# Column sums of the first norm on TensorE, and the low-rank projections moved ahead of and among the first rotations

## Chip, cores and metric

The kernel runs on one core of one Trainium2 chip. The metric is the device time of one execution in microseconds (us). The kernel before takes 2462.11 us, the median of three runs (2460.17 to 2463.86). Engines go by their short names: PE is TensorE (PEld its weight loads), DVE VectorE, ACT ScalarE, POOL GpSimd, SP the engine that issues most loads.

## The reference, cut to what matters

The model has several layers on a sequence of 512 with 1024 features: a layer of latent attention and retention, one of gated linear attention, then two more with mixtures of experts. The change lies in the first layer alone:

```python
h = _rmsnorm(x, mix_norm_even[i])
cq, ckv, k_rope, rq, rk, rv, rg = _split(h @ w_in_even[i], EVEN_SPLIT)
a = _mla(cq, ckv, k_rope, positions, ...)
r = _retention(rq, rk, rv, rg, positions, ...)
x = x + jnp.concatenate([a, r], axis=-1) @ w_out_even[i]
```

`cq` (384 features) and `ckv` (256) are the low-rank inputs of the latent attention, `k_rope` 32 more features. `rq` and `rk` are rotated by position, `rv` are the retention's values, `rg` its gates. The retention has eight heads of 64 features; its result is normed by head and multiplied by `silu(rg)`.

## The kernel before

Everything is kept as transposed tiles of 128 features by 512 positions, eight for `x`. A product of two float32 operands is made of three products of operands split in a high and a low part (`mm3`, lines 152 to 156): high by high, high by low, low by high. A weight tile of up to 128x2048 is loaded by SP into one of two `wraw` buffers, ScalarE writes its high part (`whi`, line 147, in three pieces), and VectorE or GpSimd the low part (`wlo`, line 149), in turn by the count of weights (`weight`, line 134).

A tile scheduler sets each engine's order from the order of the code, its own time line and a few hints; buffers are given out by pools. `K.u` gives one of 42 tiles of a ring, `K.h` one of four longer-lived tiles. The PSUM banks are `mm`, `tr`, `sm` and `sc`, two buffers each.

The first layer goes as follows (`layer0`, from line 458). `split_g` scales the eight tiles of `x` by the norm's gains and splits them (`xh`, `xl`). `norm_cols` (line 294) squares the tiles on ScalarE, adds the squares up on VectorE in `acc` (line 220), and `colsum` (line 222) sums `acc` over its partitions with four matmuls against a column of ones, one for each block of 128 positions. `rms_cols` makes the inverse root of it, `rc`, one number for each position. It is not applied to `x`: it goes into the rotation's table `rtab` (line 551), into the copy of the values (`ret_values`, line 531) and into a row `rb` for the gates.

`low_rank` (line 485) is a generator: five projections of 128 features (weights `w_c`), each 24 matmuls of 128x512, with a split of the result (`ch`, `cl`) and its square added to `accq` or `acck`, then `krT` of 32 features. Two of its projections are made ahead of the rotations. `ret_rows` (line 505) makes `rq`, then `rk`, in 16 blocks of 24 matmuls of 128x256: VectorE multiplies a block by cosines and sines (`xc`, `xs`, line 513), GpSimd adds them, PE transposes the result. `ret_values` has eight more blocks. `retention` (line 590) takes the heads in four pairs. For each pair it makes a decay matrix `D` for each head (GpSimd, VectorE, then an Exp on ScalarE, line 599), and in four steps the scores (`sc`, line 606), the scores by decay (`At`, line 608, VectorE) and their product with the values (`sm`, line 613). The norm of the pair follows: squares `s2` on ScalarE, a product with ones by blocks (line 618), `rsqrt_wide` (lines 194 to 204: a logarithm and an Exp on ScalarE, `rwv`, `rwt`, `rwr` on VectorE), the gated result `ro` (lines 621 and 622) and its split `ah`, `al` (lines 258 and 259).

`weave` sets generators beside each other by weights. The retention (20) is woven with the gates and what is left of `low_rank` (8), so those projections fill PE while the other engines work on a pair's norm:

```python
for _ in chain(ret_rows(0, rqT), ret_rows(1, rkT), ret_values()):
    pass
...
weave((retention(), 20), (chain(ret_gates(), low), 8))
```

Of the kernel before, what the change touches and what calls it, by code (L numbers as in the profile page):

```python
# [10 lines left out]
ACT = mybir.ActivationFunctionType  # L11
# [3 lines left out]
P = 128  # L15
# [11 lines left out]
class Ctx:  # L27
# [194 lines left out]
    def colsum(self, acc):  # L222

        ps = self.sm()
        for t in range(4):
            self.summed = self.nc.tensor.matmul(ps[:, t:t + 1], acc[:, t * P:(t + 1) * P], self.ones[:, 0:1], start=True, stop=True).ins
        return ps[:, 0:4]

    def rms_cols(self, acc, n, eps):
# [36 lines left out]
def weave(*parts):  # L266

    live = [[g, n, 0] for g, n in parts]
    while live:
        p = min(live, key=lambda p: p[2] / p[1])  # L270
        p[2] += 1
        try:
            next(p[0])
        except StopIteration:
            live.remove(p)


def chain(*gens):
    for g in gens:
        yield from g  # L280
# [12 lines left out]

def norm_cols(K, xT):

    acc = K.u("acc")
    for k in range(8):
        K.sumsq_add(acc, xT[k], k == 0)
    return K.rms_cols(acc, 1024, 1e-6)


def norm_split(K, xT, g):
# [115 lines left out]
def proj_T(K, src, n, nk, xh, xl):  # L418

    wh, wl = src if isinstance(src, tuple) else K.weight(src, nk * n * P)  # L420
    wh = wh[:, :nk * n * P].rearrange("p (k n) -> p k n", k=nk)
    wl = wl[:, :nk * n * P].rearrange("p (k n) -> p k n", k=nk)
    for j in range(n):
        ps = K.mm()
        for k in range(nk):
            K.mm3(ps, wh[:, k, j * P:(j + 1) * P], wl[:, k, j * P:(j + 1) * P], xh[k], xl[k], k == 0, k == nk - 1)
        yield ps


def proj_N(K, src, n, xh, xl):  # L430

    nk = len(xh)
    wh, wl = K.weight(src, nk * n)
    wh = wh[:, :nk * n].rearrange("p (k n) -> p k n", k=nk)
    wl = wl[:, :nk * n].rearrange("p (k n) -> p k n", k=nk)
    for t in range(4):
        s = slice(t * P, (t + 1) * P)
        ps = K.mm()[:, :n]
        for k in range(nk):
            K.mm3(ps, xh[k][:, s], xl[k][:, s], wh[:, k, :], wl[:, k, :], k == 0, k == nk - 1)  # L440
        yield t, ps


def proj_few(K, src, n, xh, xl):

    wh, wl = (w[:, :8 * n].rearrange("p (k n) -> p k n", k=8) for w in K.weight(src, 8 * n))
    ps = K.mm()[:n]
    for k in range(8):
        K.mm3(ps, wh[:, k, :], wl[:, k, :], xh[k], xl[k], k == 0, k == 7)
    return ps  # L450
# [7 lines left out]
def layer0(K, xT, A, late):  # L458
# [16 lines left out]
    late()  # L475
    xh, xl = split_g(K, xT, g)
    rc0 = norm_cols(K, xT)
    rc = c.tile([P, 4], F32, name="rc")
    V.tensor_copy(out=rc, in_=rc0)
# [5 lines left out]
    def low_rank():  # L485

        for j in range(5):
            ps, = proj_T(K, A["w_c"][j] if j else w_c0, 1, 8, xh, xl)
            h, l = K.ur("ch"), K.ur("cl")
            gg = gq[:, j:j + 1] if j < 3 else gkv[:, j - 3:j - 2]  # L490
            K.split_into(h, l, ps, gg)
            K.sumsq_add(accq if j < 3 else acck, ps, j in (0, 3))
            (cqh if j < 3 else ckh).append(h)
            (cql if j < 3 else ckl).append(l)
            yield
        V.tensor_copy(out=krT, in_=proj_few(K, A["w_kr"], 32, xh, xl))

    low = low_rank()
    for _ in range(2):
        next(low)  # L500


# [2 lines left out]
    def ret_rows(which, dst):  # L505

        for b in range(2):
            for t, ps in proj_N(K, A[("w_rq", "w_rk")[which]][b], 256, xh, xl):
                tabs = rtab[which][:, t]
                p4 = ps.rearrange("p (h b) -> p h b", b=32)  # L510
                xc, xs, xr = (K.u(n)[:, :256] for n in ("xc", "xs", "xr"))
                for o, tab in ((xc, tabs[:, 0]), (xs, tabs[:, 1])):
                    V.tensor_tensor(out=o.rearrange("p (h b) -> p h b", b=32), in0=p4, in1=tab.unsqueeze(1).to_broadcast([P, 8, 32]), op=MU)  # L513
                c4, s4, r4 = (o.rearrange("p (h a b) -> p h a b", a=2, b=32) for o in (xc, xs, xr))
                G.tensor_tensor(out=r4[:, :, 0], in0=c4[:, :, 0], in1=s4[:, :, 1], op=SU)
                x = G.tensor_tensor(out=r4[:, :, 1], in0=c4[:, :, 1], in1=s4[:, :, 0], op=AD)
                if t == 1:
                    first.setdefault("rotation", x.ins)
                pt = K.tr()
                for j in range(2):  # L520
                    nc.tensor.transpose(pt[:, j * P:(j + 1) * P], xr[:, j * P:(j + 1) * P], K.ident)
                for j in range(2):
                    d = dst[2 * b + j]
                    if which:
                        for i, r in enumerate((slice(0, 64), slice(64, P))):
                            K.copy(d[i][r, t * P:(t + 1) * P], pt[r, j * P:(j + 1) * P])
                    else:
                        K.copy(d[:, t * P:(t + 1) * P], pt[:, j * P:(j + 1) * P])
                yield

    def ret_values():
        for b in range(2):
            for t, ps in proj_N(K, A["w_rv"][b], 256, xh, xl):
                x = nc.scalar.activation(out=rv[t][:, b * 256:(b + 1) * 256], in_=ps, func=ACT.Copy, scale=rc[:, t:t + 1])
                first.setdefault("value", x.ins)
                yield

    def ret_gates():
        for b in range(2):
            for ps in proj_T(K, A["w_rg"][b], 2, 8, xh, xl):  # L540
                o = K.u("sg")
                V.tensor_tensor(out=o, in0=ps, in1=rb, op=MU)
                K.silu2(o)
                sg.append(o)
                yield
# [4 lines left out]
        for i, tab in enumerate((cos, sin)):  # L550
            V.tensor_scalar(out=rtab[0][:, t, i], in0=tab[:, t, 16:48], scalar1=rc[:, t:t + 1], scalar2=None, op0=MU)
    V.tensor_scalar(out=rtab[1], in0=rtab[0], scalar1=0.125, scalar2=None, op0=MU)
    rqT, rv = ([K.u("rT") for _ in range(4)] for _ in range(2))
    rkT = [[K.u("rk") for _ in range(2)] for _ in range(4)]
    for x, y in rkT:
        G.memset(x[64:P], 0.0)
        G.memset(y[0:64], 0.0)
    for _ in chain(ret_rows(0, rqT), ret_rows(1, rkT), ret_values()):
        pass


    th = K.load(A["theta"])
# [27 lines left out]
    def retention():  # L590
        for pair in range(4):
            Ds = []
            for h in (2 * pair, 2 * pair + 1):
                D = small.tile([P, 896], F32, tag="D", name="D")
                with K.tc.issue_after(first["rotation"]):
                    G.tensor_scalar(out=D, in0=dp, scalar1=lg[:, h:h + 1], scalar2=None, op0=MU)
                V.scalar_tensor_tensor(out=D, in0=dm, scalar=lg[:, 8 + h:9 + h], in1=D, op0=MU, op1=AD)
                with K.tc.issue_after(first["value"]):
                    nc.scalar.activation(out=D, in_=D, func=ACT.Exp)
                Ds.append(D)  # L600
            po = K.sm()
            for k in range(4):
                At = []
                for i in range(2):
                    ps = K.sc()
                    nc.tensor.matmul(ps, rkT[pair][i][:, k * P:(k + 1) * P], rqT[pair], start=True, stop=True)
                    a = K.u("At")
                    V.tensor_tensor(out=a, in0=ps, in1=Ds[i][:, 384 - 128 * k:896 - 128 * k], op=MU)
                    At.append(a)
                yield  # L610
                for i in range(2):
                    h = 2 * pair + i
                    nc.tensor.matmul(po[i * 64:(i + 1) * 64, :], rv[k][:, h * 64:(h + 1) * 64], At[i], start=k == 0, stop=k == 3)
            s2 = K.u("s2")
            nc.scalar.activation(out=s2, in_=po, func=ACT.Square)
            yield
            pn = K.mm()
            nc.tensor.matmul(pn, bo, s2, start=True, stop=True)
            r = K.rsqrt_wide(pn, 1.0 / 64, 1e-6)
            o = K.u("ro")  # L620
            V.scalar_tensor_tensor(out=o, in0=po, scalar=go[:, pair:pair + 1], in1=sg[pair], op0=MU, op1=MU)
            V.tensor_tensor(out=o, in0=o, in1=r, op=MU)
            ah[4 + pair], al[4 + pair] = K.ur("ah"), K.ur("al")
            K.split_into(ah[4 + pair], al[4 + pair], o)

    rb = K.row_bcast(rc, "rb0")
    weave((retention(), 20), (chain(ret_gates(), low), 8))


    def second(acc, n, nm):  # L630
# [10 lines left out]
    sq = second(accq, 384, "q")  # L641
# [108 lines left out]
    out = lambda half: resid_T(K, xT, A["w_out"][half], ah[half * 4:], al[half * 4:])  # L750
# [1569 lines left out]
```

## Time and profile before

| | |
|---|---|
| median of three runs | 2462.11 us (2460.17 to 2463.86) |
| profiled execution | 2463.21 us, span 2461.1 us |
| mean granted TensorE clock | 0.954 of full speed |
| busy in the span | PE 2241.3 us, DVE 1493.9, ACT 1063.8, POOL 623.0 |

The span runs from the first to the last instruction of the profiled execution; its own time has 2.1 us around that. In the timelines a row is a start, a duration and an instruction, output first; a bracket tells how long its engine was idle before it and what ended that. Rows with a count stand for several alike. Matmuls are pipelined, so durations of neighbours overlap, and the pace is the difference of starts.

### The profile page before, as it was taken

What the parts mean: (1) busy time and instruction counts of PE and PEld (TensorE: products, weight loads), DVE (VectorE), ACT (ScalarE), POOL (GpSimd) and SP (SyncE); (2) the same over time, 40 slices, a digit from 0 to 9 for tenths busy, and PEclk for the clock granted to TensorE, in tenths of its full rate; (3) what the DMA queues carried; (4) which work ended last, traced back from release to release, by engine and by line L of the source; (5) the groups of instructions that cost most, each with busy time, mean ns of one, the idle gap of its engine ahead of it and who ended that gap; (6) DMA issues with size and microseconds to landing.
All of it is one profiled execution on the core that took longest, in us unless ns stands there. A gap on an engine that the chain in (4) does not pass through costs nothing. (4 is left out here: it accounts for less than half of the span.)

```text
span 2461.1 us, 31765 instructions
## 1 busy us (share of the span) xinstructions
PE 2241.3 (91%) x12180; PEld 1820.3 (74%) x12180; DVE 1493.9 (61%) x2866; ACT 1063.8 (43%) x1796; POOL 623.0 (25%) x491
## 2 busy tenths in 40 slices
PE   7999899999999999999999999997883999997892
PEld 6944657888886888788888887576773877786782
DVE  6356865534534656896576354776766445676766
ACT  4333465323325333443243234645664444445563
POOL 6322302222222332000000021124543121124443
PEclk9999999999999999999999999997997999988996
DMA  4100201223222121332333442046884221155884
GB/s 147 70 26 32 93 1 69 98 83 114 87 83 89 69 78 52 103 112 97 135 112 103 153 145 92 35 171 212 329 314 166 95 103 69 69 197 206 305 312 162
DMA packets 71817, 306.67 MB, mean 125 GB/s; under 512 B 18048, under 2 KB 19072, under 8 KB 46048
## 3 DMA queue, kind: packets, MB, share of 16 engines
q1 hardware_dynamic: 61328, 282.29, 32.2%
q0 software_dynamic: 6912, 16.79, 2.0%
q10 hardware_dynamic: 3408, 5.39, 0.7%
q8 instruction: 100, 1.64, 0.3%
q14 instruction: 69, 0.57, 0.1%
HBM read 280.18 MB, written 32.64 MB: 127 GB/s over the span
## 5 line engine op out<-in xcount | busy, mean ns | idle before, releaser
L149 POOL TENSOR_TENSOR wlo<-wraw,whi 128x683 fp32r<-128x683 f32 (+9 forms) x233 | 427.5, 1860 | 973.2 <-ACT whi L147 922.8
L147 ACT ACTIVATE whi<-wraw 128x683 fp32r<-128x683 f32 (+9 forms) x627 | 474.7, 818 | 408.7 <-issue 135.5
L149 DVE TENSOR_TENSOR wlo<-wraw,whi 128x683 fp32r<-128x683 f32 (+9 forms) x394 | 403.4, 1059 | 110.2 <-ACT whi L147 109.7
L154 PE MATMUL mm<-xh,whi 128*128 128x512 f32 (+2 forms) x608 | 242.5, 399 | 10.0 <-ACT xh L261 8.4
L155 PE MATMUL mm<-xl,whi 128*128 128x512 f32 (+2 forms) x608 | 239.8, 394 | 0.2 <-DVE xl L262 0.2
L156 PE MATMUL mm<-xh,wlo 128*128 128x512 f32 (+2 forms) x608 | 239.2, 393 | 0.4 <-POOL wlo L149 0.3
L154 PE MATMUL mm<-whi,xh 128*128 128x256 f32 x512 | 153.0, 299 | 16.5 <-DVE xs L513 4.7
L156 PE MATMUL mm<-whi,xl 128*128 128x256 f32 x512 | 150.7, 294 | 0.0
L155 PE MATMUL mm<-wlo,xh 128*128 128x256 f32 x512 | 149.4, 292 | 0.0
L154 PEld LDWEIGHTS mm<-xh,whi 128*128 128x128 f32 (+2 forms) x608 | 113.1, 186 | 41.5 <-ACT xh L261 9.2
L156 PE MATMUL sc<-xh,wlo 128*128 128x512 f32 x352 | 137.6, 391 | 0.0
L155 PE MATMUL sc<-xl,whi 128*128 128x512 f32 x352 | 137.4, 390 | 0.0
L154 PE MATMUL sc<-xh,whi 128*128 128x512 f32 x352 | 137.0, 389 | 0.0
L162 PE MATMUL mm<-whi,Xh 128*128 128x256 f32 x512 | 131.0, 292 | 5.0 <-ACT whi L147 5.0
L155 PEld LDWEIGHTS mm<-xl,whi 128*128 128x128 f32 (+2 forms) x608 | 113.0, 186 | 29.5 <-DVE xl L262 3.2
L156 PEld LDWEIGHTS mm<-xh,wlo 128*128 128x128 f32 (+2 forms) x608 | 113.0, 186 | 27.4 <-POOL wlo L149 1.2
L163 PE MATMUL mm<-whi,Xl 128*128 128x256 f32 x512 | 128.2, 287 | 0.3
L154 PEld LDWEIGHTS mm<-whi,xh 128*128 128x128 f32 x512 | 102.2, 200 | 20.5 <-issue 9.4
L162 PEld LDWEIGHTS mm<-whi,Xh 128*128 128x128 f32 x512 | 99.3, 194 | 7.2 <-ACT whi L147 6.4
L155 PEld LDWEIGHTS mm<-wlo,xh 128*128 128x128 f32 x512 | 102.4, 200 | 0.9 <-issue 0.5
L156 PEld LDWEIGHTS mm<-whi,xl 128*128 128x128 f32 x512 | 102.3, 200 | 1.0 <-issue 0.8
L163 PEld LDWEIGHTS mm<-whi,Xl 128*128 128x128 f32 x512 | 99.2, 194 | 1.2 <-DVE Xl L259 0.9
(786 smaller groups left out, 5202.6 us busy)
## 6 DMA issues: line engine op xcount, KB each, us to landing
wraw<-in_f_up SPq DMA_DIRECT2D x44, 1024.0 KB, 4.8
wraw<-in_m_w_up SPq DMA_DIRECT2D x32, 1024.0 KB, 7.5
wraw<-in_m_w_gate SPq DMA_DIRECT2D x32, 1024.0 KB, 6.1
wraw<-in_m_w_down SPq DMA_DIRECT2D x32, 1024.0 KB, 7.4
wraw<-in_f_down SPq DMA_DIRECT2D x32, 704.0 KB, 4.0
dy<-Y SPq DMA_DIRECT2D x32, 512.0 KB, 5.1
wraw<-in_w_out SPq DMA_DIRECT2D x8, 1024.0 KB, 4.8
wraw<-in_x_out SPq DMA_DIRECT2D x8, 1024.0 KB, 4.8
```

Source lines behind the costliest of these rows:

```text
L147: nc.scalar.activation(out=hi[:, a:b], in_=raw[:, a:b], func=ACT.Copy)
L149: eng.tensor_tensor(out=lo[:, a:b], in0=raw[:, a:b], in1=hi[:, a:b].bitcast(F32), op=ALU.subtract)
L154: nc.tensor.matmul(out, ahi, bhi, start=first, stop=False)
L155: nc.tensor.matmul(out, ahi, blo, start=False, stop=False)
L156: nc.tensor.matmul(out, alo, bhi, start=False, stop=last)
L162: nc.tensor.matmul(out, a[k][0], b[k][0], start=k == 0, stop=False)
L163: nc.tensor.matmul(out, a[k][1], b[k][0], start=False, stop=False)
```

## The change

Three edits. The eight squares of the first norm each stay in a tile of their own, and `colsum` sums over tiles as well, with 32 accumulating matmuls. Three low-rank projections precede the rotations instead of two, a fourth is woven in among them, and the weave with the retention holds the last one and `krT`. The four tiles of the retention's values come from `K.h`, where the latent attention's values are put later, and no more from the ring.

```diff
     def colsum(self, acc):
 
         ps = self.sm()
+        acc = acc if isinstance(acc, list) else [acc]
         for t in range(4):
-            self.summed = self.nc.tensor.matmul(ps[:, t:t + 1], acc[:, t * P:(t + 1) * P], self.ones[:, 0:1], start=True, stop=True).ins
+            for k, a in enumerate(acc):
+                self.summed = self.nc.tensor.matmul(ps[:, t:t + 1], a[:, t * P:(t + 1) * P], self.ones[:, 0:1], start=k == 0,
+                                                    stop=k == len(acc) - 1).ins
         return ps[:, 0:4]
...
 def norm_cols(K, xT):
 
-    acc = K.u("acc")
+    sq = [K.u("sq") for _ in range(8)]
     for k in range(8):
-        K.sumsq_add(acc, xT[k], k == 0)
-    return K.rms_cols(acc, 1024, 1e-6)
+        K.nc.scalar.activation(out=sq[k], in_=xT[k], func=ACT.Square)
+    return K.rms_cols(sq, 1024, 1e-6)
...
     low = low_rank()
-    for _ in range(2):
+    for _ in range(3):
         next(low)
...
-    rqT, rv = ([K.u("rT") for _ in range(4)] for _ in range(2))
     rkT = [[K.u("rk") for _ in range(2)] for _ in range(4)]
     for x, y in rkT:
         G.memset(x[64:P], 0.0)
         G.memset(y[0:64], 0.0)
-    for _ in chain(ret_rows(0, rqT), ret_rows(1, rkT), ret_values()):
-        pass
+    rqT, rv = [K.u("rT") for _ in range(4)], [K.h("rv") for _ in range(4)]
+    weave((chain(ret_rows(0, rqT), ret_rows(1, rkT), ret_values()), 24), (islice(low, 1), 2))
...
-    weave((retention(), 20), (chain(ret_gates(), low), 8))
+    weave((retention(), 20), (chain(ret_gates(), low), 6))
```

`islice(low, 1)` takes one projection from the generator. Line numbers of the changed kernel are higher by 1 to 5.

PE, the column sum. Before, the four matmuls stand behind the second projection and ahead of the first rotation block (128x256):

```order
L154 MATMUL mm<-xh,whi 128x512
L155 MATMUL mm<-xl,whi 128x512
L156 MATMUL mm<-xh,wlo 128x512
L226 MATMUL sm<-ones,acc 128x1 x4
L154 MATMUL mm<-whi,xh 128x256
L155 MATMUL mm<-wlo,xh 128x256
L156 MATMUL mm<-whi,xl 128x256
```

In the changed kernel they stand at the end of the first projection, and two more projections follow:

```order
L155 MATMUL mm<-xh,whi 128x512
L229 MATMUL sm<-ones,sq 128x1
L156 MATMUL mm<-xl,whi 128x512
L157 MATMUL mm<-xh,wlo 128x512
L229 MATMUL sm<-ones,sq 128x1 x31
L155 MATMUL mm<-xh,whi 128x512
L156 MATMUL mm<-xl,whi 128x512
L157 MATMUL mm<-xh,wlo 128x512
```

The sum moved ahead of the second projection. The two further projections have 48 matmuls; behind the first rotation block stand the 24 of a fourth.

VectorE, between the first and the second pair of heads. Before:

```order
L597 SCALAR_TENSOR_TENSOR D<-dm,lg,D 128x896
L203 SCALAR_TENSOR_TENSOR rwr<-rwt,rwr 128x512
L622 TENSOR_TENSOR ro<-ro,rwr 128x512
L259 TENSOR_TENSOR al<-ro,ah 128x512
L608 TENSOR_TENSOR At<-sc,D 128x512 x2
L542 TENSOR_TENSOR sg<-mm,rb_1253 128x512
```

In the changed kernel:

```order
L601 SCALAR_TENSOR_TENSOR D<-dm,lg,D 128x896
L203 SCALAR_TENSOR_TENSOR rwt<-rwt,rwv 128x512
L204 SCALAR_TENSOR_TENSOR rwr<-rwt,rwr 128x512
L626 TENSOR_TENSOR ro<-ro,rwr 128x512
L263 TENSOR_TENSOR al<-ro,ah 128x512
L612 TENSOR_TENSOR At<-sc,D 128x512 x4
L547 TENSOR_TENSOR sg<-mm,rb_1356 128x512
```

`At` stands directly behind `al` in both; four in a row instead of two. On PE, 24 matmuls of a gate projection stand between the product of line 618 (now 622) and the first use of that `At`, where 48 stood before; between the third and the fourth pair it is the 24 of `krT` alone, where 24 of the last projection preceded them. Between the second and the third pair it is 48 in both.

ScalarE, in the same place. Before:

```order
L615 ACTIVATE s_1374<-sm 128x512
L198 ACT_TABLE_LOAD
L198 ACTIVATE rwr<-mm,eps_188 128x512
L200 ACT_TABLE_LOAD
L200 ACTIVATE rwr<-rwr 128x512
L599 ACTIVATE D<-D 128x896 x2
L258 ACTIVATE ah<-ro 128x512
```

In the changed kernel:

```order
L619 ACTIVATE s_1477<-sm 128x512
L199 ACT_TABLE_LOAD
L199 ACTIVATE rwr<-mm,eps_209 128x512
L603 ACT_TABLE_LOAD
L603 ACTIVATE D<-D 128x896
L201 ACTIVATE rwr<-rwr 128x512
L603 ACTIVATE D<-D 128x896
L262 ACTIVATE ah<-ro 128x512
```

The first Exp of `D` moved ahead of that of `rwr`; the same holds between the third and the fourth pair.

## Rows read from the trace of the kernel before

**Rows 1.** Page, part 1: busy us (share of the span) and instructions.
```profile
PE 2241.3 (91%) x12180; PEld 1820.3 (74%) x12180; DVE 1493.9 (61%) x2866; ACT 1063.8 (43%) x1796; POOL 623.0 (25%) x491
```

**Rows 2.** PE's waits from 0 to 300 us: line, releaser, total, times, longest.
```profile
PE mm L154 <- DVE xs L513: 4.7, 3, 1.8
...
PE mm L618 <- ACT s L615: 0.7, 1, 0.7
PE mm L156 <- POOL wlo L149: 0.3, 1, 0.3
PE mm L154 <- DVE rwv L199: 0.2, 1, 0.2
```

**Rows 3.** Timeline of PE, 18 to 28 us: start, us, instruction, [idle before, releaser].
```profile
18.59 0.50 PE L154 MATMUL mm<-xh,whi 128*128 128x512 f32 x1 [1.60 <-ACT whi L147]
...
21.68 0.39 PE L154 MATMUL mm<-xh,whi 128*128 128x512 f32 x1
...
25.10 0.94 PE L226 MATMUL sm<-ones,acc 128*128 128x1 f32 x8
27.82 0.58 PE L154 MATMUL mm<-whi,xh 128*128 128x256 f32 x1 [1.77 <-ACT accq L216]
```

**Rows 4.** Windows: us, busy by engine, clock, DMA share, GB/s.
```profile
28.00:31.00 3.00, 3.00 (x15) 3.00 (x16) 0.60 (x1) 2.98 (x5) 3.00 (x9) 0.50 0.74 306
38.00:41.00 3.00, 3.00 (x16) 3.00 (x15) 0.00 (x0) 0.00 (x0) 1.46 (x4) 0.50 0.05 22
1621.00:1622.00 1.00, 1.00 (x10) 1.00 (x10) 0.62 (x2) 0.54 (x1) 0.00 (x0) 0.87 0.56 141
1622.00:1628.00 6.00, 6.00 (x18) 4.94 (x19) 0.53 (x3) 0.00 (x0) 0.00 (x0) 0.50 0.95 331
```

**Rows 5.** Timeline of VectorE, 24 us: the last add of the squares.
```profile
24.13 0.68 DVE L220 TENSOR_TENSOR acc<-acc,sq 128x512 f32<-128x512 f32 x1
```

**Rows 6.** Timeline of ScalarE: the squares.
```profile
14.42 3.74 ACT L219 ACTIVATE sq<-xT 128x512 f32<-128x512 f32 x7
```

**Rows 7.** Timeline of PE, 1618 to 1629 us: narrow products, then wide ones.
```profile
1618.16 1.51 PE L1720 MATMUL sm<-pk 128*128 128x20 f32 x12
1619.61 1.09 PE L793 MATMUL sm<-PT,fv 128*64 128x128 f32 x14
1620.63 2.62 PE L1722 MATMUL sm<-m0wg,ones 128*128 128x20 f32 x16
1623.08 0.77 PE L154 MATMUL mm<-whi,ah 128*128 128x512 f32 x1
...
1628.34 0.50 PE L155 MATMUL mm<-wlo,ah 128*128 128x512 f32 x1
```

**Rows 8.** Timeline of PE, 233 to 240 us: after the wait for `ah`.
```profile
233.07 0.79 PE L154 MATMUL mm<-ah,whi 128*128 128x512 f32 x1 [2.97 <-ACT ah L258]
...
239.08 0.52 PE L155 MATMUL mm<-wlo,ch 128*128 128x512 f32 x1
```

**Rows 9.** Timeline of PE, retention, end of pair 0 and start of pair 1.
```profile
139.62 1.02 PE L618 MATMUL mm<-s,bo 128*128 128x512 f32 x2
...
151.48 1.07 PE L613 MATMUL sm<-At,rT 128*64 128x512 f32 x2
```

**Rows 10.** Timeline of VectorE in the same place.
```profile
148.44 0.69 DVE L259 TENSOR_TENSOR al<-ro,ah 128x512 fp32r<-128x512 f32 x1 [0.70 <-ACT ah L258]
149.05 1.28 DVE L608 TENSOR_TENSOR At<-sc,D 128x512 f32<-128x512 f32 x2
```

**Rows 11.** Timeline of ScalarE in the same place.
```profile
142.74 0.63 ACT L200 ACTIVATE rwr<-rwr 128x512 f32<-128x512 f32 x1
143.27 0.94 ACT L599 ACTIVATE D<-D 128x896 f32<-128x896 f32 x1
```

**Rows 12.** Timeline of PE, retention, start of pair 3.
```profile
208.07 1.07 PE L613 MATMUL sm<-At,rT 128*64 128x512 f32 x2
```

**Rows 13.** Timeline of VectorE in the same place.
```profile
206.12 1.28 DVE L608 TENSOR_TENSOR At<-sc,D 128x512 f32<-128x512 f32 x2
```

More of the change, by code (lines that the diff above doesn't have):

```diff
@@ L1 @@
 from contextlib import ExitStack
+from itertools import islice
 import numpy as np
```

## The prediction

> **What bounds the kernel now.** The first view is the page's busy times [rows 1]: TensorE (PE) works 2241.3 of 2461.1 us, no other engine above 61%. A microsecond of PE work that is added costs one unless it lies in a PE wait, and one taken away returns only if PE then has something to do. So the question is where PE waits, and the change touches nothing behind some 230 us: after the retention the rows of every engine stand as before. The second view is the list of PE's waits up to 300 us [rows 2] and PE's timeline of the first norm [rows 3]. From the end of the first low-rank projection (low0) PE waits 1.60 us for a weight half, then 1.77 for ScalarE to clear a bank; behind them three waits on `xs` of the rotations, 4.7 in all. Behind these, up to the one that ends at 233.07 [rows 8], it waits only twice more, 0.7 and 0.2 us. The third is the granted clock in windows [rows 4]: 0.50, the lower of its two levels (1.2 and 2.4 GHz), from 28 and from 38 us, behind waits of 1.8 us.
>
> **The column sum.** Seven adds of 0.68 us leave VectorE [rows 5]. They lie in front of the sum and PE did not wait for the last of them: it was busy with the second projection (low1) until 25.10 [rows 3]. I cost their removal at nothing. TensorE gets 32 small products in place of 4; each f32 product is two passes in the trace, eight for four [rows 3], so 64 pairs of weight load and 128x1 matmul in place of 8. They now stand directly behind low0. The squares set the pace at first: ScalarE ends the last one at about 18.2 [rows 6], and PE waited there until 18.59 anyway; 16 pairs go into that. That leaves 48 pairs from 18.3 on. What does a pair take? Nearest are the narrow 128x20 products late in the program [rows 7]: 12 of them from 1618.16 to 1619.61, with two others among them, 0.11 each. There the clock fell, although PE had no gap, at about 1621.7 [rows 4], 3.6 us after the narrow work began; the last six of the 16 pairs from 1620.63 then took to 1623.08, about 0.22 each. The eight pairs of the sum before, 0.94 us, are also near 0.11 [rows 3], too few to show a fall. Bounds: 48 x 0.11 = 5.3, ending at 23.6; 48 x 0.22 = 10.6, ending at 28.9. I take what the nearest rows show: 21 pairs to the fall at about 20.6, and 27 x 0.22 = 5.9, ending at **26.5**.
>
> **The first stretch.** A projection is 24 products at 0.228 us (15 from 21.68 to 25.10 [rows 3]), 5.5 us. After the narrow work, wide products started at half clock and came back 5.4 us later [rows 7]; after waits it took 3.3 and 3.4 us (3.0 in full windows [rows 4] and some tenths at either end) and 6.2 us [rows 8]. Half of each is lost: 2.7, 1.6, 1.7 and 3.1. I take their mean, 2.3, for every such stretch, with 1.6 and 3.1 as its ends. So low1 ends at 26.5 + 5.5 + 2.3 = 34.3 and low2 at 39.8, where the rotations start; before they started at 27.82 [rows 3]. That is +12.0. From there to the end of the first eight blocks of rotations, low3 is added (+5.5). The `xs` waits go (-4.7), because the root and the tables, which made the first one, are done some 9 us before PE needs them now and because low3 gives VectorE 5.5 us to catch up; with them go two half-clock stretches (1.6 + 1.7). What is late next is the bank of low3: ScalarE takes it only after a transpose copy that stands before it, about 1.0 us more. Together 12.0 + 5.5 - 4.7 - 3.3 + 1.0 = **+10.5**; between +4.3 (sum at 0.11, no half clock in low1, no bank wait) and +15.2 (0.22 throughout, 3.1 in low1, one `xs` wait of 1.5 stays).
>
> **Retention.** Two of five low-rank projections leave it, 48 products, 11.0 us. Not the wave of steps itself changes but the filler between two pairs of heads: 24 products in place of 48 between pairs 0 and 1, and between 2 and 3. PE reached pair 1 at 151.48 without a wait [rows 9]; now it would be there at 146.0. But the first product of pair 1 needs `At`, and VectorE makes it behind the whole norm of pair 0: `al` at 148.44, then two `At` from 149.05, the first done at 149.7 [rows 10]. The slack was 151.48 - 149.7 = 1.8 us, not 5.5. In the new order ScalarE's Exp of `D`, 0.94 us, stands ahead of the Exp of `rwr` [rows 11], so the chain is later by about that, and `At` comes at about 150.7: a new wait of 4.7, a gain of 0.8. Between pairs 2 and 3 the slack was 208.07 - 206.8 = 1.3, with the first `At` again 0.68 behind its start [rows 12, 13]; the same swap and the copy of `krT` ahead of `At` take it: gain 0. The extremes are 1.8 + 1.3 gained, or nothing. Each new wait is longer than the 2.97 us behind which the clock stayed low 6.2 us [rows 8], so each is followed by half clock in steps that keep PE full: 2 x 2.3. Retention gives -0.8 + 4.6 = **+3.8**.
>
> **The rest.** The retention values in the `h` tiles change the place of four tiles, not their writer (ScalarE) or readers; nothing in the trace waits for a unit of the ring that they leave: 0. The swap of halves between VectorE and GpSimd that follows from the new sequence of weights goes with the first stretch; the GpSimd half that low1 needs was 0.3 us late before [rows 2], and the column sum now covers it. On SP two more loads of 0.5 MB stand ahead of the first rotation weights; at the 306 GB/s of 28 to 31 us [rows 4] that is 3.4 us, and the rotations start 12 us later: 0.
>
> **Sum.** +10.5 + 3.8 = +14.3 on the profiled execution's 2463.2: 2477.5. That execution stood 1.1 above the median of the three runs, so **2476**. The unknown costs alone reach from +4.4 (4.3 - 3.1 + 3.2) to +21.4 (15.2 + 6.2), 2466 to 2483.
>
> **A rule against one term.** Rows 7 show pairs that took twice as long once the clock was at half. The Trainium skill, in "TensorE: Matmul & The Clock Gate", section "LDWEIGHTS (loading the stationary operand)", gives a weight load as its columns divided by 1.2, in ns, with no clock in it: 107 ns for 128 columns. By that rule the 48 pairs would take an estimated 5.1 us in either state. The first 12 pairs of rows 7 agree with it, the last six do not.
>
> **Rivals.** (1) *The pairs keep 0.11.* For it: the short sums of today do; against it: the last six pairs of [rows 7]. The sum then ends at 23.6, not 26.5: 2473.5; if the clock does not fall either, low1 saves its 2.3: 2471. (2) *The moved 11.0 us come back in full, faster.* One place, the wait of pairs 1 and 3 for `At`: if VectorE made `At` ahead of `ro` and `al`, PE could run on at 146.0 and 202.6 at full clock. Then -11.0 takes the place of +3.8; it decides against me wherever the first stretch costs less than 6.1. With rival 1 on top that is 5.3, so 2456. The order of VectorE's rows speaks against it: `At` stands behind `al` in both kernels. (3) *The same with the slow sum*: 10.5 - 11.0, 2461.6, no change; the same verdict if the first stretch is hidden in some way I don't see, as by weight loads that PE did not wait for in this trace. (4) *All at the upper bounds*: 2483.
>
> **How the numbers follow.** About 0.2%, 4.9 us, is what a measurement of this kernel tells from no change. Forecast 0.48; rival 1 0.19; rival 2 0.11; rival 3 0.16; rival 4 0.06. Forecast, rival 1 and rival 4 are slower: 0.73. Rival 3 is the same: 0.16. Rival 2 is faster: 0.11. The range takes in the other three and leaves out rival 2: 2460 to 2483. The likeliest case's own range is 2466 to 2483.
>
> **What would show it.** Right: a row of 64 matmuls of the column sum that ends near 26.5, with windows of clock 0.50 from about 20.6 to the middle of low1; the first rotation near 39.8; the end of the first eight blocks some 10 us later; PE's list of waits with two on `At` of 4 to 6 us and a clock of 0.50 behind each; the last step of retention some 14 us later. Wrong: column-sum rows at 0.11 to the end (rival 1); no waits on `At` (rivals 2 and 3), the first thing I would look for; `xs` waits still there, which adds up to 4.7.

## The result and the profile after

The change makes the kernel slower: 2483.51 us, the median of four runs (2482.63 to 2485.99), against 2462.97 (2460.17 to 2463.86) for the kernel before in the same comparison. The ratio is 1.0082, with a 95% interval of 1.007 to 1.0093. The direction was forecast; the size was not: +20.5 us where +14 was expected, and the time lies half a microsecond above the range's upper end. The profiled execution is the slowest of the four (2485.99 us, span 2484.2).

PE's busy time rose by 17.1 us against [rows 1]. The column sum is some 11 of that (12.3 us in place of 0.94), and most of the rest is work at half clock. The other engines stayed nearly where they were:

```profile
PE 2258.4 (91%) x12236; PEld 1832.9 (74%) x12236; DVE 1487.4 (60%) x2859; ACT 1063.6 (43%) x1796; POOL 621.4 (25%) x491
```

The list of PE's waits from 0 to 320 us (line, releaser, total, times, longest), which answers to [rows 2], has a new entry:

```profile
PE sm L617 <- DVE At L612: 11.7, 2, 7.1
```

It stands for two waits on `At`. The waits of the first stretch fell from 8.4 us (4.7, 1.77, 1.60 and 0.3 in [rows 2, 3]) to 3.2 (0.48, 1.09 and 1.64 in the timeline below). They did not all go.

PE's timeline through the first stretch, which answers to [rows 3]. The first row is all of the column sum but its first two pairs. The next two are the start of low1 and the row in which the clock returned, then the first rotation, and the three waits:

```profile
16.38 12.32 PE L229 MATMUL sm<-ones,sq 128*128 128x1 f32 x62
28.56 0.77 PE L155 MATMUL mm<-xh,whi 128*128 128x512 f32 x1
...
32.12 0.60 PE L157 MATMUL mm<-xh,wlo 128*128 128x512 f32 x1
...
41.45 0.28 PE L155 MATMUL mm<-whi,xh 128*128 128x256 f32 x1
...
44.96 0.50 PE L155 MATMUL mm<-xh,whi 128*128 128x512 f32 x1 [0.48 <-ACT sq L220]
...
54.86 0.39 PE L155 MATMUL mm<-whi,xh 128*128 128x256 f32 x1 [1.09 <-ACT acck L217]
...
72.02 0.36 PE L155 MATMUL mm<-whi,xh 128*128 128x256 f32 x1 [1.64 <-DVE xs L518]
```

Windows of the same execution; the number before the last two is the granted clock, as in [rows 4]:

```profile
17.00:18.50 1.50, 1.23 (x9) 0.98 (x9) 0.95 (x5) 1.50 (x4) 0.00 (x0) 1.00 0.00 0
18.50:19.00 0.50, 0.50 (x6) 0.50 (x6) 0.00 (x0) 0.50 (x3) 0.24 (x1) 0.91 0.00 0
19.00:28.50 9.50, 9.50 (x46) 9.50 (x47) 3.38 (x4) 6.26 (x12) 6.00 (x19) 0.50 0.47 167
28.50:32.50 4.00, 4.00 (x10) 3.18 (x11) 2.51 (x17) 0.26 (x1) 0.00 (x0) 0.50 0.00 0
...
164.50:169.00 4.50, 4.48 (x5) 1.08 (x6) 1.03 (x2) 0.00 (x0) 0.00 (x0) 0.50 0.00 0
225.00:233.50 8.50, 8.50 (x16) 3.46 (x16) 1.96 (x8) 0.00 (x0) 4.47 (x9) 0.50 0.20 62
```

The clock fell to its lower level at 18.9, 2.5 us after the narrow products began (PE was idle for 0.27 us of that, between 17.0 and 18.5), and stayed there to the end of the sum and 4 us into low1. From 19.0 to 28.5 there are 46 pairs in 9.5 us, 0.21 each. The two other stretches stand behind the waits on `At`.

PE's timeline of the retention, the product with ones that ends a pair and the first use of `At` in the next, which answer to [rows 9, 12]:

```profile
153.39 1.02 PE L622 MATMUL mm<-s,bo 128*128 128x512 f32 x2
...
164.52 1.97 PE L617 MATMUL sm<-At,rv 128*64 128x512 f32 x2 [4.65 <-DVE At L612]
...
211.29 1.02 PE L622 MATMUL mm<-s,bo 128*128 128x512 f32 x2
...
224.95 1.94 PE L617 MATMUL sm<-At,rv 128*64 128x512 f32 x2 [7.09 <-DVE At L612]
...
246.11 1.12 PE L622 MATMUL mm<-s,bo 128*128 128x512 f32 x2 [0.69 <-ACT s L619]
```

In the kernel before, three of these instructions are in [rows 9, 12] (139.62, 151.48 and 208.07); the other two are:

```profile
196.10 1.02 PE L618 MATMUL mm<-s,bo 128*128 128x512 f32 x2
...
225.03 1.13 PE L618 MATMUL mm<-s,bo 128*128 128x512 f32 x2 [0.75 <-ACT s L615]
```

From these starts follows where the time went:

| stretch of PE | before | after | difference |
|---|---|---|---|
| to the end of pair 0 | 139.62 | 153.39 | +13.8 |
| gap between pairs 0 and 1 | 11.86 | 11.13 | -0.7 |
| pair 1, the next gap, pair 2 | 44.62 | 46.77 | +2.2 |
| gap between pairs 2 and 3 | 11.97 | 13.66 | +1.7 |
| pair 3 | 16.96 | 21.16 | +4.2 |
| sum, end of pair 3 | 225.03 | 246.11 | +21.1 |

Some 2 us of that come back in the attention that follows, where PE waits 3.2 us for `qT` instead of 4.6. The span of this execution is 23.1 us longer than that before all the same: some 4 us more are lost behind 2200 us, in code that the change leaves alone. All of this compares one execution of each kernel. Executions of the same instructions differ here: of the runs below, e6 and e8 have the changed kernel's order on PE up to the end of pair 0 and reach it at 152.24 and 151.98, 1.2 and 1.4 us before the 153.39 of the table.

### The profile page after: what moved, and what is told of

The parts are those of the page before. It is cut to its first block, busy times and chain, and to the rows that moved or that the text cites. A ratio compares the mean times of both kernels' runs of the same rounds, so it can differ in the third digit from the quotient of the medians.

```text
span 2484.2 us, 31864 instructions
## 1 busy us (share of the span) xinstructions
PE 2258.4 (91%) x12236; PEld 1832.9 (74%) x12236; DVE 1487.4 (60%) x2859; ACT 1063.6 (43%) x1796; POOL 621.4 (25%) x491
## 5 line engine op out<-in xcount | busy, mean ns | idle before, releaser
L155 PE MATMUL mm<-whi,xh 128*128 128x256 f32 x512 | 151.3, 296 | 12.3 <-DVE gqk L901 5.0
L155 PEld LDWEIGHTS mm<-whi,xh 128*128 128x128 f32 x512 | 100.4, 196 | 16.9 <-issue 5.4
```

The lines of the kernel that those rows point to most:

```text
L155: nc.tensor.matmul(out, ahi, bhi, start=first, stop=False)
```

## The experiments

Each comparison has its own runs of the kernel before (medians of 2463.9 to 2464.8). All times are medians, ratios are to that kernel.

**The squares added on VectorE again (e1_old_sum).**

```diff
-    sq = [K.u("sq") for _ in range(8)]
+    acc = K.u("acc")
     for k in range(8):
-        K.nc.scalar.activation(out=sq[k], in_=xT[k], func=ACT.Square)
-    return K.rms_cols(sq, 1024, 1e-6)
+        K.sumsq_add(acc, xT[k], k == 0)
+    return K.rms_cols(acc, 1024, 1e-6)
```

> The changed kernel with one part undone: the squares are added up on VectorE again and four small matmuls sum the one tile; the order of the projections and the retention's filler stay as changed. Theory A (the column sum is dear as a whole: 12.3 us of narrow pairs, of which about 2 lie in a wait that is there anyway, and 2 us of half clock in the projection behind it): the rotations start about 9.8 us earlier than in the changed kernel, the retention is as in it: 2473 to 2475. Rival B (the sum is cover for waits that come back when it goes, on the root and the tables): the rotations start earlier but wait for xs, under 4 us in all: 2480 or more.

Measured: 2486.16 us, ratio 1.0084 (1.0067 to 1.0101). My theory fell: with the 12-us column sum gone the kernel is no faster than with it. Rival B's time held, but the waits that came are not on `xs`. PE's timeline shows them, ahead of low1 and of low3, and the start of the rotations:

```profile
18.60 0.79 PE L155 MATMUL mm<-xh,whi 128*128 128x512 f32 x1 [2.36 <-ACT whi L148]
...
32.51 0.39 PE L155 MATMUL mm<-whi,xh 128*128 128x256 f32 x1
...
39.63 0.80 PE L155 MATMUL mm<-xh,whi 128*128 128x512 f32 x1 [3.99 <-ACT sq L220]
```

VectorE's timeline says why the second is so long. Behind the root it makes the tables, then a weight half, and only then `cl` of low2, on which ScalarE's `sq` waits that frees the bank:

```profile
36.40 0.63 DVE L557 TENSOR_SCALAR rtab<-rtab 128x256 f32<-128x256 f32 x1
36.95 1.34 DVE L150 TENSOR_TENSOR wlo<-wraw,whi 128x341 fp32r<-128x341 f32 x3
38.21 0.74 DVE L266 SCALAR_TENSOR_TENSOR cl<-mm,pk,ch 128x512 fp32r<-128x512 f32 x1
```

With the later two (1.09 and 1.64, as in the changed kernel) the waits of this stretch are 9.1 us, more than the 8.4 before the change. The rotations start 8.9 us earlier than in the changed kernel, near the 9.8 expected, but most of that goes again. The wait ahead of low3 is 3.5 longer, and behind it PE runs 6.2 us at half clock, of which half is lost: together 6.6 of the 8.9. The end of pair 0 is at 150.95, 2.4 earlier than in the changed kernel and 11.3 later than before: the two moved projections cost their whole 11.0 us, and filled nothing.

**The column sum on TensorE alone (e2_sum_only).** The kernel before with `colsum` and `norm_cols` as in the change.

```diff
-    acc = K.u("acc")
+    sq = [K.u("sq") for _ in range(8)]
     for k in range(8):
-        K.sumsq_add(acc, xT[k], k == 0)
-    return K.rms_cols(acc, 1024, 1e-6)
+        K.nc.scalar.activation(out=sq[k], in_=xT[k], func=ACT.Square)
+    return K.rms_cols(sq, 1024, 1e-6)
```

> The kernel before with the column sum on TensorE alone. Theory A: the sum ends near 28.5 and the second projection runs partly at half clock, so the rotations start some 8 us later than before; in return the waits on xs that came from the late root and one half-clock stretch go, 4 to 5 us. Net +3 to +5: 2466 to 2468; the retention is as before, no wait on At. Rival B (the sum hides nothing): +8 to +10, 2471 to 2473. Rival C (the sum is cheap, the loss came from the moved projections): within 2 of before.

Measured: 2466.82 us, ratio 1.0017 (1.0006 to 1.0029), in theory A's range, though not by its terms. The rotations start at 34.38 instead of 27.82, 6.6 later and not 8; at the end of pair 0 5.3 of that is left (144.95), so 1.3 came back where theory A had 4 to 5; the medians differ by 2.9. Alone the sum costs a little; beside the moved projections it costs nothing that the medians show, because most of it stands where they would wait.

**The retention values in the four tiles alone (e3_values_only).**

```diff
-    rqT, rv = ([K.u("rT") for _ in range(4)] for _ in range(2))
+    rqT, rv = [K.u("rT") for _ in range(4)], [K.h("rv") for _ in range(4)]
```

> The kernel before with the retention values in the four longer-lived tiles alone. Theory A: nothing waits for these tiles, the time is that of before, 2461 to 2465. Rival: the scheduler takes the first steps of pair 0 ahead of the last values and changes what fills PE: more than 3 us either way.

Measured: 2462.81 us, ratio 0.9996 (0.9986 to 1.0006): no change, as the prediction had it.

**Filler placed by hand, first try (e4_fill).** A `yield` behind the product with ones, and the weave written out:

```diff
             nc.tensor.matmul(pn, bo, s2, start=True, stop=True)
+            yield
             r = K.rsqrt_wide(pn, 1.0 / 64, 1e-6)
...
-    weave((retention(), 20), (chain(ret_gates(), low), 6))
+    r, f = retention(), chain(ret_gates(), low)
+    for n in (0, 2, 2, 2):
+        for _ in range(n):
+            next(f, None)
+        for _ in range(6):
+            next(r, None)
+    for _ in chain(f, r):
+        pass
```

> The changed kernel with the filler of the retention put elsewhere: none among the steps of pair 0, 48 products in each of the three gaps between pairs (the same number in all). Theory A (the loss in the retention is that of gaps of 24 products, shorter than the norm's chain of some 11 us, and of the half clock behind each): the two waits on At and both half-clock stretches go, 11.0 us of filler leave pair 0 and fill the gaps: about -18 against the changed kernel, 2464 to 2468. Rival B (the steps of pair 0 need the filler as cover for decay matrices and At): new waits in pair 0, 2473 to 2480. Rival C (the gap's end is set by At in either case): no gain, 2483.

Measured: 2507.70 us, ratio 1.0174 (1.0156 to 1.0192). A miss, by my own edit. Pair 0 needs no cover: it ends at 142.38, 11.0 earlier than in the changed kernel, just its filler. But the gates now precede the norm in the code, and ScalarE's timeline shows the norm's logarithm (L199) behind both tanh of the gates (L210), 16.9 us after `s`, where it was 1.9 in the changed kernel:

```profile
141.52 0.60 ACT L619 ACTIVATE s<-sm 128x512 f32<-128x512 f32 x1 [11.75 <-PE sm L617]
...
156.46 0.61 ACT L210 ACTIVATE sl<-sg 128x512 f32<-128x512 f32 x1
...
158.39 0.69 ACT L199 ACTIVATE rwr<-mm,eps 128x512 f32<-128x512 f32 x1
```

PE's list has three waits on `At`, 24.1 us. The run says nothing against the theory of the gaps, nor for it.

**Three projections ahead, filler by hand (e5_three).** Squares as before, no projection among the rotations, the same `yield` and loop with (1, 2, 2, 2).

```diff
-    weave((chain(ret_rows(0, rqT), ret_rows(1, rkT), ret_values()), 24), (islice(low, 1), 2))
+    for _ in chain(ret_rows(0, rqT), ret_rows(1, rkT), ret_values()):
+        pass
...
+    for n in (1, 2, 2, 2):
```

> VectorE adds up the squares as before; three low-rank projections precede the rotations, none stands among them; the filler of the retention is set by hand: 24 products among the steps of pair 0, 48 in each of the three gaps. Theory D (a gap between pairs ends when the norm's chain gives At, some 11.5 us, and takes 48 products for nothing; products among the steps of pair 0 cost their full time): all gaps stay as before, pair 0 is 5.5 shorter. The moved projection costs 5.5 ahead of the rotations at most, less where it fills a wait: 2459 to 2464, no wait on At over 1 us. Rival (gates in another gap than before make the norm's chain late): waits on At, 2468 or more.

Measured: 2506.44 us, ratio 1.0174 (1.0157 to 1.0191). The same fault (the norm's logarithm 16.6 us behind `s`), and waits on `At` of 25.0 us. One thing can be read all the same, since it lies ahead of the retention: the second rotation block waits 5.05 us for low2's `sq`. The third projection in this place filled no wait either.

**Work added to the changed kernel (e6_again).** Two projections are computed once more, unused, so that each gap has 48 products again.

```diff
+    def again():
+        for j in (2, 3):
+            for _ in proj_T(K, A["w_c"][j], 1, 8, xh, xl):
+                yield
+
     rb = K.row_bcast(rc, "rb0")
-    weave((retention(), 20), (chain(ret_gates(), low), 6))
+    weave((retention(), 20), (chain(ret_gates(), again(), low), 8))
```

> The changed kernel with work added: two of the low-rank projections are computed a second time in the retention and not used, so that the filler there is as before the change, 48 products in every gap. Theory D: 48 more products, 11.0 us of TensorE work, cost nothing, since they take the place of two waits of 11.7 us in all, and both stretches of half clock (2.2 and 4.2) go: 2476 to 2480, faster than the changed kernel with less work. Rival: added work costs its length, the waits are not what they seem: 2490 to 2495.

Measured: 2477.87 us, ratio 1.0055 (1.0039 to 1.0072). With 11 us more TensorE work the kernel is 5.6 us faster than the changed one; against its own runs of the kernel before it loses 13.0 us instead of 20.5. PE's timeline has no wait on `At`; the gaps are 11.86 and 11.97 us as before the change, and pair 3 takes 16.90 (from 220.69 to 237.59):

```profile
152.24 1.02 PE L622 MATMUL mm<-s,bo 128*128 128x512 f32 x2
...
164.10 1.07 PE L617 MATMUL sm<-At,rv 128*64 128x512 f32 x2
...
208.72 1.02 PE L622 MATMUL mm<-s,bo 128*128 128x512 f32 x2
...
220.69 1.07 PE L617 MATMUL sm<-At,rv 128*64 128x512 f32 x2
...
237.59 1.12 PE L622 MATMUL mm<-s,bo 128*128 128x512 f32 x2 [0.69 <-ACT s L619]
```

What is left of the loss, 13 us, is the first stretch's: the end of pair 0 and that of pair 3 are both 12.6 later than before.

**Half of the column sum (e7_half_sum).**

```diff
         K.nc.scalar.activation(out=sq[k], in_=xT[k], func=ACT.Square)
-    return K.rms_cols(sq, 1024, 1e-6)
+        if k % 2:
+            K.nc.vector.tensor_tensor(out=sq[k - 1], in0=sq[k - 1], in1=sq[k], op=ALU.add)
+    return K.rms_cols(sq[::2], 1024, 1e-6)
```

> The changed kernel with half of the column sum: VectorE adds the squares in four pairs, TensorE sums four tiles with 16 small products instead of 32. Theory A (the narrow pairs lie on the path): 32 pairs fewer at 0.2 us, -6 against the changed kernel, 2477 to 2479. Theory F (the sum covers waits for the root, the tables and the banks behind VectorE, as in the run without it): the rotations start earlier, but a wait of the fourth projection for its bank takes most of it back: 2481 to 2486.

Measured: 2483.63 us, ratio 1.0077 (1.006 to 1.0094): the same as with all of it. It is neither theory's mechanism: 32 pairs fewer, but the sum now waits for VectorE's adds three times, 2.7 us in all, the last 1.43:

```profile
21.38 5.71 PE L229 MATMUL sm<-ones,sq 128*128 128x1 f32 x26 [1.43 <-DVE sq L304]
```

The first rotation starts at 39.34, 2.1 us earlier than in the profile of the changed kernel, and pair 0 ends 2.1 earlier (151.28); no wait of low3 took that. But against e6 and e8, which have the whole sum, pair 0 ends only 1.0 and 0.7 earlier, less than executions of the same instructions differ. So the 2.1 are mostly the execution's, which is in line with the equal medians.

**No GpSimd split beside the norm of pair 2 (e8_no_gpsimd).** One run.

```diff
-def proj_T(K, src, n, nk, xh, xl):
+def proj_T(K, src, n, nk, xh, xl, eng=None):
...
-    wh, wl = src if isinstance(src, tuple) else K.weight(src, nk * n * P)
+    wh, wl = src if isinstance(src, tuple) else K.weight(src, nk * n * P, eng)
...
-        for d, ps in enumerate(proj_T(K, w[b], 4, 4, ah, al)):
+        for d, ps in enumerate(proj_T(K, w[b], 4, 4, ah, al, K.nc.vector)):
```

> The changed kernel with the low parts of the output projection's weights made by VectorE, so that GpSimd splits none while VectorE works on the norm of pair 2. Theory: ro and al of pair 2, which took 2.08 and 1.34 us beside GpSimd, take 0.7 each again, and the wait of pair 3 for At falls from 7.1 to about 5.0. Rival: they stay long, since something else holds VectorE there; the wait stays at 7.

Measured: 2480.66 us, too few to tell from the changed kernel. The changed kernel's timelines of VectorE and GpSimd in the gap between pairs 2 and 3:

```profile
220.10 2.08 DVE L626 TENSOR_TENSOR ro<-ro,rwr 128x512 f32<-128x512 f32 x1
222.87 1.34 DVE L263 TENSOR_TENSOR al<-ro,ah 128x512 fp32r<-128x512 f32 x1 [0.70 <-ACT ah L262]
224.13 1.27 DVE L612 TENSOR_TENSOR At<-sc,D 128x512 f32<-128x512 f32 x2
```

```profile
220.00 5.70 POOL L150 TENSOR_TENSOR wlo<-wraw,whi 128x682 fp32r<-128x682 f32 x3 [8.87 <-ACT whi L148]
```

and VectorE's in this run:

```profile
218.51 0.85 DVE L150 TENSOR_TENSOR wlo<-wraw,whi 128x682 fp32r<-128x682 f32 x1
219.29 0.67 DVE L626 TENSOR_TENSOR ro<-ro,rwr 128x512 f32<-128x512 f32 x1
219.89 1.63 DVE L150 TENSOR_TENSOR wlo<-wraw,whi 128x683 fp32r<-128x683 f32 x2
221.45 0.67 DVE L263 TENSOR_TENSOR al<-ro,ah 128x512 fp32r<-128x512 f32 x1
```

`ro` and `al` are back at 0.67, so GpSimd's split had held them, by 2.1 us together. The changed kernel says the same by itself: between pairs 0 and 1, where GpSimd has no work, both took 0.69. The Trainium skill, "SBUF — State Buffer", section "SBUF: two separate sides", has the rule: GpSimd, and a VectorE instruction with two inputs in SBUF, lock the same ports for a whole instruction. The rows agree: `At`, whose one input is in PSUM, took its 0.64 beside GpSimd. The wait for `At` fell only to 6.49, not to 5.0, since the split's 2.48 us now stand in VectorE's own order:

```profile
222.87 1.94 PE L617 MATMUL sm<-At,rv 128*64 128x512 f32 x2 [6.49 <-DVE At L612]
```

**The filler moved from pair 0 into the gap (e10_filler_moved).** The changed kernel; the filler follows a pair's norm in the code, as the weave has it.

```diff
-    weave((retention(), 20), (chain(ret_gates(), low), 6))
+    r, f = retention(), chain(ret_gates(), low)
+    for i in range(20):
+        for _ in range({0: 1, 6: 2, 11: 2, 16: 1}.get(i, 0)):
+            next(f, None)
+        next(r, None)
+    for _ in chain(f, r):
+        pass
```

> The changed kernel with the retention's filler placed by hand in the order that the weave gave: 24 products among the steps of pair 0 instead of 48, 48 in the gap between pairs 0 and 1 instead of 24; the gap between pairs 2 and 3 keeps its 24. Theory D: pair 0 is 5.5 us shorter, the gap grows by 0.8 and its wait and half clock go (-2.2): -7 against the changed kernel, 2475 to 2478; one wait on At of 7 is left. Rival (the filler's place does not matter, only its sum): 2483.

Measured: 2477.57 us, ratio 1.0057 (1.0039 to 1.0074). The time is as expected, its terms only in part. In PE's timeline the gap between pairs 0 and 1 is 11.88 us without a wait, and from pair 1 to pair 2 PE takes 44.62 us as before the change. But pair 0 is 4.0 shorter, not 5.5, since its first product now waits 1.45 for `At`. Between pairs 2 and 3 the wait is still there:

```profile
133.06 1.07 PE L617 MATMUL sm<-At,rv 128*64 128x512 f32 x2 [1.45 <-DVE At L612]
...
149.44 1.02 PE L622 MATMUL mm<-s,bo 128*128 128x512 f32 x2
...
161.32 1.07 PE L617 MATMUL sm<-At,rv 128*64 128x512 f32 x2
...
218.91 1.94 PE L617 MATMUL sm<-At,rv 128*64 128x512 f32 x2 [6.40 <-DVE At L612]
...
237.82 1.13 PE L622 MATMUL mm<-s,bo 128*128 128x512 f32 x2 [0.69 <-ACT s L619]
```

Pair 3 then took 18.91 us instead of 21.16, which the edit did not aim at. Without this luck the time would have come out some 2 us higher.

**One projection moved, to where PE waits (e9_one_among, e11_one_values).** The kernel before; one projection behind the first rotation block, the filler as in the run above with one more step behind the last pair's first scores. The second run has the values in the four tiles besides.

```diff
-    for _ in chain(ret_rows(0, rqT), ret_rows(1, rkT), ret_values()):
-        pass
+    weave((chain(ret_rows(0, rqT), ret_rows(1, rkT), ret_values()), 24), (islice(low, 1), 1))
...
+        for _ in range({0: 1, 6: 2, 11: 2, 16: 2}.get(i, 0)):
```

> The kernel before with one projection moved, and to another place: it stands behind the first rotation block, where TensorE waited for the tables; the retention's filler is 24 products among the steps of pair 0 and 48 in each of the three gaps, in the order of the code that the weave gave. Theory D: the gaps stay as before without a wait on At, pair 0 is 5.5 us shorter; ahead of it the projection costs 5.5 less what it fills: the second block waits for the tables (37.4) instead of the third, +2.9, and a stretch of half clock may go, -1.7. Sum -2.6 to -4.3 against before: 2460 to 2462. Rival (its bank waits behind the tables too, as in the run without the sum on TensorE): 2465 or more.

> As the run with one projection among the rotations, with the retention values in the four longer-lived tiles as well. Those tiles alone gave -1.1, within the noise. Theory: the same time as that run, 2459 to 2462. Rival: the new place of the steps of pair 0 costs or gains over 3 us.

Measured: 2462.46 us, ratio 0.9992 (0.9984 to 1.0001), and 2460.00, ratio 0.999 (0.9979 to 1.0001). The first is half a microsecond above its range, the second inside it. Both lie below the kernel before, neither beyond what can be told from no change. PE's timelines show the last product of the sixteen rotation blocks (the 384th of 128x256) in the kernel before and in e9, and then a wait of e9:

```profile
87.75 0.28 PE L156 MATMUL mm<-whi,xl 128*128 128x256 f32 x1
```

```profile
88.57 0.28 PE L157 MATMUL mm<-whi,xl 128*128 128x256 f32 x1
...
120.08 1.07 PE L613 MATMUL sm<-At,rT 128*64 128x512 f32 x2 [1.45 <-DVE At L608]
```

With 5.5 us more work ahead of it, this product is 0.8 later than before: the projection filled what the wait for the tables had left open. (Against e3, whose projections stand as before, it is 2.2 later.) Pair 0 gave back less than 5.5, since its first product waits 1.45 for `At`, and it ends at 136.45, 3.2 earlier than before. The profiled execution of e9 is among its fastest, 3.7 us below its median. The clock is no evidence here: it is 1.00 from 28 to 31 and from 38 to 41 us in e9, where [rows 4] have 0.50, but it is so in e3 too.

## Why the prediction was right in its direction and wrong in its size

**The column sum** was put on the path at 26.5 as the pace of all that follows. Its mechanism held: narrow pairs, a fall of the clock under them, 0.21 a pair from there (0.22 expected), low1 at half clock for 4 us, half of it lost (2.0; 2.3 expected). The size was off: the clock fell 2.5 us after the narrow work began, not 3.6, and the sum ended at 28.5. That is 2.0 of the first stretch's miss in this execution. Other executions of the same instructions differ, as the first row of low1 in e6 and in e10 shows:

```profile
26.84 0.77 PE L155 MATMUL mm<-xh,whi 128*128 128x512 f32 x1
```

```profile
29.16 0.77 PE L155 MATMUL mm<-xh,whi 128*128 128x512 f32 x1
```

So the forecast's 26.5 lies just below what was seen, and the 2.0 are in part this execution's. As a cause the term was misplaced. Taking the sum out (e1) or halving it (e7) gives nothing that the medians show: without it the moved projections wait 5.9 us longer (9.1 against 3.2) and lose 3.1 to half clock. Rival 1, which made the pace of the pairs decide, priced the wrong thing.

**"The `xs` waits go (-4.7)"** is the step that failed in the first stretch. One of 1.64 stayed, as the upper bound allowed. The step gave all three waits one cause, the late root and tables. But the third of them was another matter, and it is the one that stayed: it comes 2.9 us ahead of the ninth rotation block in both kernels, and in both VectorE has just stood idle, 2.2 and 2.3 us, for ScalarE's copy `rT` of a transposed block. Before the change it was:

```profile
58.26 0.35 PE L154 MATMUL mm<-whi,xh 128*128 128x256 f32 x1 [1.49 <-DVE xs L513]
```

A wait of 0.48 for low2's bank was not in the sum; the 1.0 for low3's bank was (1.09). With the sum's 2.0, and with low1 and low2 shorter by 0.4 than forecast, that is 3.8; the stretch came out 3.3 above the forecast (13.8 against 10.5). The other 0.5 is not accounted for. The price of the moved projections was right: 11.0, and e1 shows them at 11.3.

**The retention's mechanism was right**, and e6 and e10 show it: the gap between pairs 0 and 1 ended 0.7 earlier, 0.8 expected; its wait was 4.65, 4.7 expected; the half clock behind it cost 2.2, 2.3 expected. **The gap between pairs 2 and 3 was mis-sized.** "Gain 0" was a loss of 1.7: in the new order GpSimd splits a weight there, and holds `ro` and `al` of VectorE by 2.1 us (e8). I had followed the order of VectorE and ScalarE in that gap and not GpSimd's. And "2 x 2.3" met a stretch of at least 8.5 us at half clock behind the longer wait: 4.2 lost in pair 3. Nearly the same wait cost less in e10, 6.40 and 1.95 lost, and as much as here in e8, 6.49 and 4.4; why the stretch differs by that much is not settled. In all, the retention lost 7.4 where 3.8 was forecast.

**The range** reached 2483, and the time is 2483.5. The sum of its upper bounds, +21.4 on 2462.1, is 2483.5 too, written half a microsecond short. Its upper end did hold the first stretch (+15.2) but took the retention as never worse than 6.2, with no loss in the second gap; at 7.4 that bound was not one.

**What took the loss apart**: e6 puts 13 us on the first stretch and the rest, some 7, on the two short gaps. Of the three edits the projections are the loss: with the values and the old sum they alone cost 22 (e1), the sum alone 2.9 (e2), the values nothing (e3).

## What to carry to other kernels

A filler that covers a chain of other engines is free up to that chain's length, so taking it away gives back only the slack behind it; compare the chain's end with the filler's end before moving it. A wait is filled by new work only if that work's own needs (here its bank, freed by the engine that everybody waited for) are met while the wait lasts: in e9's profile the place behind the first block did that, in e1's and e5's the place ahead of it did not. Waits that name the same tile can have different causes; each has to be followed to its own. To test whether a stretch is bound by a chain, add work to it: if the kernel gets no slower, or faster as in e6, the added work lies off the path there. And one profile of a kernel is one execution: here two of the same instructions differ by 1.4 us at the end of pair 0.

## What the runs showed of the hardware

TensorE's clock fell while the engine had no gap. e6 shows it most plainly: its column sum starts at 17.53, PE is busy without a break, and the clock goes from 1.00 to 0.50 between 21.5 and 22.0:

```profile
16.50:21.00 4.50, 4.50 (x39) 4.33 (x38) 2.61 (x11) 4.48 (x12) 2.19 (x3) 1.00 0.00 0
...
21.50:22.00 0.50, 0.50 (x5) 0.50 (x5) 0.50 (x1) 0.50 (x1) 0.22 (x1) 0.68 0.00 0
22.00:26.80 4.80, 4.80 (x24) 4.80 (x24) 1.27 (x3) 3.33 (x6) 3.33 (x16) 0.50 0.65 232
```

In the changed kernel 46 pairs of 128x128 weight load and one-column product filled the 9.5 us from 19.0 to 28.5 completely, at 0.50. The time of a pair then was 0.21 us, twice the 0.11 at full clock [rows 7]. The Trainium skill, "TensorE: Matmul & The Clock Gate", section "LDWEIGHTS (loading the stationary operand)", divides a load's columns by 1.2 to get its ns, an estimated 107 ns here, with no clock in the formula; the rows of the changed kernel do not agree with that as the price of a pair at half clock, so the measurement decides.
